# Routing from pairs of score columns, and dense loads tied to the gathers, in a two-layer attention and expert kernel

## The chip, the cores and the metric

One core of a Trainium2 chip runs the whole kernel. The metric is the device time of one execution in microseconds, as a median over runs. Engines are named as in the profile: PE (matmul), PEld (its weight load), DVE, ACT, POOL, SP (which only issues DMAs here).

## The reference

Two layers over 256 tokens of width 1024, float32. Each layer has a norm, attention and a gated short convolution, merged and projected, and then `peer`, which holds most of the bytes:

```python
q = (hf @ w_query).reshape(T, 8, 2, 128)
scores = einsum("thpd,hpnd->thpn", q, sub_keys)          # two score columns of 128 keys per head
top_v, top_i = top_k(scores, 16)
cand_v = top_v[:, :, 0, :, None] + top_v[:, :, 1, None, :]
cand_i = top_i[:, :, 0, :, None] * 128 + top_i[:, :, 1, None, :]
best_v, best_pos = top_k(cand_v.reshape(T, 8, 256), 16)
expert_idx = take_along_axis(cand_i, best_pos)           # 128 experts of 16384 per token
gates = softmax(best_v)
a = gelu(einsum("td,thkd->thk", h, expert_u[expert_idx]))
out = einsum("thk,thkd->td", gates * a, expert_v[expert_idx])
```

The output of the second layer is normed once more.

## The kernel before

The 256 tokens are two blocks of 128, block 0 and block 1 (`t` in the code). The expert stage (`experts`) does them in two ways at once.

**Block 0, dense.** All 16384 rows of `expert_u` and then of `expert_v` are streamed through SBUF, 64 MiB each. "An expert" in the loops is a group of 128 rows; a load brings a pair of them, 1 MiB. The U loop multiplies each pair with the hidden state (L1079) and leaves gelu values in `halves` (tiles `al` and `ah`). `weigh` makes one-hot tiles from the transposed factors iT, jT and gT (POOL, ACT and DVE, L1048 to L1052), multiplies them on PE (L1066), and scales `halves` with the result on DVE (L1068). The V loop multiplies `halves` with each pair of V (L1124), into two PSUM tiles that collect over all 128 steps. `factors` makes iT, jT and gT with three PE transposes (L889) and three DVE copies; their PSUM tile has two buffers.

**Block 1, gathered.** For each of a token's 128 experts one indirect DMA on POOL's queue (L977) brings a row per token, 128 x 1024 (0.52 MB): 128 gathers from U and 128 from V, in the order of GROUPS. They land in 8 row buffers (9 in the first and 11 in the second layer from the middle of the V loop on). `use` consumes the oldest: DVE, L993 for U (dot product with the token's h) or L1001 for V (adds to y1), and the freed buffer is gathered into at once. A group can be gathered when its indices are routed.

**Routing** (`route`, a generator in the list `bg`) is some 17 us of DVE per block and quarter of the heads: MAX, MAX_INDEX and MATCH_REPLACE over four score columns of 128 keys (L825 to L829), the sums (L835), a second search (L842 to L846), and one-hot products that give indices (L851 to L873). `route_all` does block 1's four quarters, then block 0's, then the shares and `factors`. `query` makes 16 units of the queries on PE (L926), the scores of a unit one unit later (L911), and after every fourth unit ACT copies four score columns of each block from PSUM to `s4` (L916) and hands them to `route_all`.

**The order of the work** is the order in which the program is written: each engine does its instructions in that order and waits on semaphores. `fill(budget)` lets `route_all` go on by so much estimated time per step of the query and U loops, with a credit of at most 3000. In the V loop the number of uses per step is set so that the remaining gathers fall evenly to LAST = 10 at the end.

**Loads.** `load_ahead` issues the next load of `stream` on SP's queue as soon as the program has a free buffer for it: one of three `raw` buffers, or, for the query weights and U, spare parts of tiles that are not yet in use (`al`, `ah`, `rows`, `hot`). SP then waits until the buffer's last reader is done. The stream goes on without a break into the weights of the next layer.

After the V loop, `update` adds y times a gate row to x for block 0, the last ten gathers are used, then `update` for block 1, the transposes of x for the next layer (`turn_x`), and in the second layer the final norm and output per block.

## Time and profile before

| what | us |
| --- | --- |
| median of 3 runs | 1887.41 (1883.96 to 1890.22) |
| the profiled execution, its own time | 1891.51 |
| its span | 1889.7 |
| busy: PE / DVE / POOL / ACT | 1610.9 / 1404.6 / 889.1 / 572.9 |
| bytes moved | 669.21 MB, mean 354 GB/s over the span |

The span has a part for each layer. Layer 0: mixing until about 255, query and routing from there, the U loop from about 325 to 623, the V loop to 926, the rest until 970. Layer 1 repeats it: query from about 1178, U loop to about 1550, V loop to 1847, end at 1889.7. Busy time of an engine is a share over all these stages. A stage is read by what was late in it: the rate of the DMA engines in a stretch, and the wait ahead of an instruction, which stands in brackets behind its row with the instruction that ended it.

### The profile page before, as it was taken

The page shows a single profiled execution, that of the slowest core. Times are in us where ns is not written, and L with a number is a line of the kernel's source. Part 1 is how long each engine was busy: PE and PEld are TensorE (multiplying, and loading weights), DVE is VectorE, ACT ScalarE, POOL GpSimd, SP SyncE. Part 2 cuts the span into 40 slices and gives each one's busy share as a digit, 9 for nine tenths or more (in the row PEclk, how much of TensorE's full clock was granted, in tenths as well). Part 3 has the DMA queues.
Part 4 walks back from the last instruction along what each step waited for, and adds up shares of the span by engine and source line. Part 5 has one row for each costly group of instructions (what it writes and reads, how often), then busy time and mean ns, then how long its engine had stood idle before and what let it go on. Part 6 is the DMA issues. An engine that isn't in the chain of part 4 may idle for free.

```text
span 1889.7 us, 25904 instructions
## 1 busy us (share of the span) xinstructions
PE 1610.9 (85%) x9524; PEld 1261.0 (67%) x9527; DVE 1404.6 (74%) x2603; ACT 572.9 (30%) x1241; POOL 889.1 (47%) x731
## 2 busy tenths in 40 slices
PE   6798889978589999899559999999785999997990
PEld 4688768978589755433247997899775995453330
DVE  7897848999988766643586967499999885666338
ACT  3464232111166444200045444121113654440001
POOL 3424203444488745544551231144436985555443
PEclk7999989989889999899879999999887999998995
DMA  8658787999999999999935677799999999999995
GB/s 317 247 208 301 268 333 291 404 408 408 400 354 400 412 416 416 409 415 417 412 132 200 238 298 260 295 397 409 409 409 352 404 403 416 416 415 415 417 416 230
DMA packets 162960, 669.21 MB, mean 354 GB/s; under 512 B 15761, under 2 KB 15761, under 8 KB 146450
## 3 DMA queue, kind: packets, MB, share of 16 engines
q1 hardware_dynamic: 87106, 396.39, 53.7%
q0 software_dynamic: 73856, 268.48, 35.9%
q10 hardware_dynamic: 1872, 2.69, 0.5%
q8 instruction: 75, 1.23, 0.3%
q14 instruction: 51, 0.42, 0.1%
HBM read 666.46 MB, written 1.05 MB: 353 GB/s over the span
## 4 chain that ended last, share of the span: by engine, by line
DMA 34%; DVE 30%; PE 22%; issue 5%; POOL 2%; ACT 2%; POOLq 0%; DVEq 0%; ACTq 0%; SPq 0%
DMA rows<-in_expert_v_dram,idx 20%; DMA rows<-in_expert_rows_dram,idx 11%; PE mm L1079 8%; DVE rows L993 7%; DVE y L1001 6%; PE mm L926 3%; PE wp L1066 3%; DVE raw L280 2%; DVE wl L335 2%; PE mm L384 1%; PE mm L385 1%; PE mm L386 1%; POOL rows L977 1%; DMA raw<-in_w_gt_dram 1%; DVE ti L826 1%
## 5 line engine op out<-in xcount | busy, mean ns | idle before, releaser
L1001 DVE SCALAR_TENSOR_TENSOR y<-rows,cv,y 128x1024 f32<-128x1024 f32 x254 | 337.4, 1328 | 198.1 <-DMA rows<-in_expert_v_dram,idx 190.3
L977 POOL DMA_INDIRECT rows<-in_expert_rows_dram,idx x256 | 287.7, 1124 | 359.8 <-DVE rows L993 133.3
L977 POOL DMA_INDIRECT rows<-in_expert_v_dram,idx x256 | 304.2, 1188 | 317.6 <-DMA rows<-in_expert_v_dram,idx 137.2
L993 DVE SCALAR_TENSOR_TENSOR rows<-rows,h 128x1024 f32<-128x1024 f32 x256 | 325.4, 1283 | 73.9 <-DMA rows<-in_expert_rows_dram,idx 66.3
L335 POOL TENSOR_TENSOR wl<-raw,wh 128x1024 fp32r<-128x1024 f32 x52 | 134.3, 2587 | 258.6 <-ACT wh L330 249.3
L1079 PE MATMUL mm<-hfull,raw 128*128 128x128 f32 x1984 | 242.2, 282 | 15.0 <-ACT al L1093 15.0
L1124 PE MATMUL yp<-raw,ah 128*128 128x512 f32 x512 | 239.1, 612 | 17.7 <-DMA raw<-in_expert_v_dram 14.8
L1079 PEld LDWEIGHTS mm<-hfull,raw 128*128 128x128 f32 x1984 | 234.2, 197 | 15.8 <-ACT al L1093 15.8
L1124 PE MATMUL yp<-raw,al 128*128 128x512 f32 x512 | 237.5, 607 | 2.1 <-DMA raw<-in_expert_v_dram 2.0
L1051 ACT ACTIVATE hot<-iotf,iT 128x128 f32<-128x128 f32 x512 | 163.3, 390 | 200.8 <-PE wp L1066 175.1
L1079 PE MATMUL mm<-hfull,ah 128*128 128x128 f32 x1600 | 193.7, 283 | 31.6 <-ACT al L1093 23.6
L1079 PEld LDWEIGHTS mm<-hfull,ah 128*128 128x128 f32 x1600 | 189.5, 199 | 32.8 <-ACT al L1093 24.3
L1124 PEld LDWEIGHTS yp<-raw,ah 128*128 128x128 f32 x512 | 94.2, 193 | 160.9 <-issue 97.7
L1066 PEld LDWEIGHTS wp<-hot 128*128 128x128 f32 x1024 | 131.4, 196 | 60.7 <-POOL hot L1049 39.6
L384 PE MATMUL mm<-hh,wh 128*128 128x256 f32 x512 | 149.9, 293 | 14.0 <-ACT gt L770 6.1
L1124 PEld LDWEIGHTS yp<-raw,al 128*128 128x128 f32 x512 | 93.5, 193 | 99.8 <-issue 94.8
L1066 PE MATMUL wp<-hot 128*128 128x64 f32 x1024 | 133.5, 274 | 27.2 <-POOL hot L1049 27.1
L330 ACT ACTIVATE wh<-raw 128x1024 fp32r<-128x1024 f32 x112 | 116.1, 1053 | 113.9 <-DMA raw<-in_w_gt_dram 47.6
L385 PE MATMUL mm<-hl,wh 128*128 128x256 f32 x512 | 146.3, 286 | 0.0
L386 PE MATMUL mm<-hh,wl 128*128 128x256 f32 x512 | 146.2, 286 | 0.0
L1049 POOL TENSOR_TENSOR hot<-hot,gT 128x256 f32<-128x256 f32 x128 | 137.3, 1073 | 2.3
L335 DVE TENSOR_TENSOR wl<-raw,wh 128x1024 fp32r<-128x1024 f32 x60 | 91.3, 1531 | 41.2 <-ACT wh L330 40.3
(229 smaller groups left out, 2345.3 us busy)
## 6 DMA issues: line engine op xcount, KB each, us to landing
raw<-in_expert_v_dram SPq DMA_DIRECT2D x128, 1024.0 KB
raw<-in_expert_u_dram SPq DMA_DIRECT2D x62, 1024.0 KB
ah<-in_expert_u_dram SPq DMA_DIRECT2D x50, 1024.0 KB
raw<-in_w_adat_dram SPq DMA_DIRECT2D x64, 512.0 KB
raw<-in_w_gt_dram SPq DMA_DIRECT2D x16, 1024.0 KB
raw<-in_w_adag_dram SPq DMA_DIRECT2D x16, 1024.0 KB
raw<-in_w_cv_dram SPq DMA_DIRECT2D x12, 1024.0 KB
raw<-in_w_qk_dram SPq DMA_DIRECT2D x8, 1024.0 KB
```

Of the source, the lines that this page charges most:

```text
L335: l_engine().tensor_tensor(lo, raw, f(h), op=OP.subtract)
L384: T.matmul(ps, h[:, c], mh[:, k], start=first, stop=False)
L385: T.matmul(ps, h[:, c], ml[:, k], start=False, stop=False)
L386: T.matmul(ps, lo[:, c], mh[:, k], start=False, stop=last)
L977: G.indirect_dma_start(out=t, out_offset=None, in_=rows[kind], in_offset=bass.IndirectOffsetOnAxis(ap=idx[:, s:s + 1], axis=0))
L993: V.scalar_tensor_tensor(t, t, 1.0, h1, op0=OP.mult, op1=OP.mult, accum_out=av[:, s:s + 1])
L1001: V.scalar_tensor_tensor(y1, t, cv[:, s:s + 1], y1, op0=OP.mult, op1=OP.add)
L1049: G.tensor_tensor(q, q, gT[:, ts, None].to_broadcast([128, TB, 64]), op=OP.mult)
L1051: A.activation(p[:, i], iotf, AF.Abs, bias=iT[:, b * TB + i:b * TB + i + 1])
L1066: T.matmul(ps[:, t], p[:, t], q[:, t], start=True, stop=True)
L1079: T.matmul(ps[:, u + x], raw[:, x, k * 128:(k + 1) * 128], hf[:, k, :128], start=(k == 0), stop=(k == KD - 1))
L1124: T.matmul(ys[q], halves[i // 64][:, i % 64], raw[:, x, q * 512:(q + 1) * 512], start=(i == 0), stop=(i == NE - 1))
```

## The change

Five edits, all in or around `experts`.

- `query` collects scores in PSUM tiles of two columns, copies them after every second unit, and hands `route_all` the tile with its first two columns. `route` does these two, then yields until the other two are there (`whole`).
- `fill` has a credit of 4000; the query loop gives 3600 per step before step 9 and 2400 from there on (2600 before).
- Between the shares and `factors` of block 0 the generator yields eight more times.
- While gathers are left (`in_step`), each V load of the stream is preceded by a DVE memset of one element and a DMA of one element over it on SP's queue, so that SP comes to the load only when DVE has come to the memset.
- All gathers are used by step 122 of the V loop; block 1 is then updated (and in the second layer normed and put out), and block 0 last. `turn_x` takes block 1 first.

```diff
-LAST = 10
+LAST = 122
...
+    in_step = {"on": False, "n": 0, "marks": cst.tile([1, DEPTH * NE // 2], F32, name="marks")}
...
+            if kind == "V" and in_step["on"]:
+
+                mark = in_step["marks"][0:1, in_step["n"]:in_step["n"] + 1]
+                in_step["n"] += 1
+                V.memset(mark, 0.0)
+                nc.sync.dma_start(mark, d["c"][:, 0:1])
             for s, ap in parts:
                 nc.sync.dma_start(t[:, s], ap)
...
-        credit[0] = min(credit[0] + budget, 3000.0)
+        credit[0] = min(credit[0] + budget, 4000.0)
...
         for i in range(4):
+            while i == 2 and not whole():
+                yield None
             s = s4[:, i]
...
         def score(n, qs):
+            if n % 2 == 0:
+                for t in range(NT):
+                    banks[t] = w_ps([128, 2, 128])
             if n % 4 == 0:
-                for t in range(NT):
-                    banks[t] = w_ps([128, 4, 128])
                 banks["k"] = keys.popleft()
...
-            if n % 4 == 3:
+            if n % 2:
                 for t in (1, 0):
-                    s4 = pool.tile([128, 4, 128], F32, name=f"sc{t}", bufs=4 - 2 * t)
-                    A.activation(s4, banks[t], AF.Copy)
-                    got(t, n // 4, s4)
+                    if n % 4 == 1:
+                        s4s[t] = pool.tile([128, 4, 128], F32, name=f"sc{t}", bufs=4 - 2 * t)
+                    A.activation(s4s[t][:, n % 4 - 1:n % 4 + 1], banks[t], AF.Copy)
+                    got(t, n // 4, s4s[t], n % 4 == 3)
...
             shares(rp, sel[0], slice(0, 8))
             yield 600
+            for _ in range(8):
+                yield None
             factors(sel[0], iT, jT, gT)
...
-            fill(2600)
+            fill(3600 if n < 9 else 2400)
...
+        def finish_block(t, last_t):
+            update(tail, ys, row, t, xg, last_t)
+            if xg:
+                y, ops = rstd_ops(t, t + 1)
+                for op in ops:
+                    op()
+                scale(xg[0], t, y, V, A)
...
-                while len(tasks) + len(flying) > LAST + (left - LAST) * (1 - (i + 1) / NE):
+                while len(tasks) + len(flying) > left * (1 - (i + 1) / LAST):
                     if not flying:
                         break
                     use()
+                in_step["on"] = bool(tasks or flying)
                 tick()
             dense_done()
-        xg = None
-        if fg is not None:
-            xg = tail.tile([128, NT, D], F32, name="xg"), fg
+            if e == LAST:
+                assert not flying
+                finish_block(1, 0)
         pol["pool"] = 1.0
-        for t in range(NT):
-            while t and flying:
-                use()
-            update(tail, ys, row, t, xg, 1)
...
+        finish_block(0, 0)
...
-        xps = None if xg else turn_x()
+        xps = None if xg else turn_x((1, 0))
```

**DVE around the factors of block 0, layer 0.** `sel` holds the routed factors and gates, `y` is y1; a row with `y` is one use of a V gather. Before:

```order
644 L867 TENSOR_REDUCE sel_2402<-oh 128x32
645 L1001 SCALAR_TENSOR_TENSOR y_2407<-rows_2326,cv,y_2407 128x1024
646 L1001 SCALAR_TENSOR_TENSOR y_2407<-rows_2323,cv,y_2407 128x1024
647 L1001 SCALAR_TENSOR_TENSOR y_2407<-rows_2324,cv,y_2407 128x1024
648 L1001 SCALAR_TENSOR_TENSOR y_2407<-rows_2325,cv,y_2407 128x1024
649 L1001 SCALAR_TENSOR_TENSOR y_2407<-rows_2326,cv,y_2407 128x1024
650 L881 TENSOR_REDUCE sm<-sel_2402 128x8
651 L882 RECIPROCAL sm<-sm 128x8
652 L883 TENSOR_TENSOR sel_2402<-sel_2402,sm 128x128
653 L893 TENSOR_SCALAR iT<-wp 128x128
654 L891 COPY jT<-wp 128x128
655 L891 COPY gT<-wp 128x128
```

With the change, from the shares on:

```order
645 L891 TENSOR_REDUCE sm<-sel_2403 128x8
646 L892 RECIPROCAL sm<-sm 128x8
647 L893 TENSOR_TENSOR sel_2403<-sel_2403,sm 128x128
648 L1013 SCALAR_TENSOR_TENSOR y_2408<-rows_2327,cv,y_2408 128x1024
649 L1013 SCALAR_TENSOR_TENSOR y_2408<-rows_2324,cv,y_2408 128x1024
650 L1013 SCALAR_TENSOR_TENSOR y_2408<-rows_2325,cv,y_2408 128x1024
651 L1013 SCALAR_TENSOR_TENSOR y_2408<-rows_2326,cv,y_2408 128x1024
652 L1013 SCALAR_TENSOR_TENSOR y_2408<-rows_2327,cv,y_2408 128x1024
653 L1013 SCALAR_TENSOR_TENSOR y_2408<-rows_2324,cv,y_2408 128x1024
654 L1013 SCALAR_TENSOR_TENSOR y_2408<-rows_2325,cv,y_2408 128x1024
655 L1013 SCALAR_TENSOR_TENSOR y_2408<-rows_2326,cv,y_2408 128x1024
656 L903 TENSOR_SCALAR iT<-wp 128x128
```

The copies of the factors stand behind eight more uses; from the start of routing there are 87 uses ahead of them before, and 90 now. On PE the three transposes stand behind 83 experts of the U loop (eight products each). Before:

```order
1322 L1079 MATMUL mm<-hfull,ah 128x128 x48
1323 L1079 MATMUL mm<-hfull,raw 128x128 x40
1324 L889 MATMUL wp<-ident,sel_2402 128x128 x3
1325 L1079 MATMUL mm<-hfull,raw 128x128 x8
1326 L1079 MATMUL mm<-hfull,ah 128x128 x8
1327 L1066 MATMUL wp<-hot 128x64 x4
```

With the change:

```order
1322 L1097 MATMUL mm<-hfull,ah 128x128 x48
1323 L1097 MATMUL mm<-hfull,raw 128x128 x48
1324 L1097 MATMUL mm<-hfull,ah 128x128 x8
1325 L899 MATMUL wp<-ident,sel_2403 128x128 x3
1326 L1097 MATMUL mm<-hfull,ah 128x128 x16
1327 L1084 MATMUL wp<-hot 128x64 x4
```

They stand behind 85 experts with the change, two more.

**DVE at the end of layer 0.** `tmp<-yp` and the row behind it are the update of block 0, `tmp<-y` that of block 1. Before, from the last row of the update of block 0 on:

```order
950 L442 TENSOR_TENSOR xt<-xt,tmp 128x512
951 L1001 SCALAR_TENSOR_TENSOR y_2407<-rows_2323,cv,y_2407 128x1024
952 L1001 SCALAR_TENSOR_TENSOR y_2407<-rows_2324,cv,y_2407 128x1024
953 L1001 SCALAR_TENSOR_TENSOR y_2407<-rows_2325,cv,y_2407 128x1024
954 L1001 SCALAR_TENSOR_TENSOR y_2407<-rows_2326,cv,y_2407 128x1024
955 L1001 SCALAR_TENSOR_TENSOR y_2407<-rows_2323,cv,y_2407 128x1024
956 L1001 SCALAR_TENSOR_TENSOR y_2407<-rows_2324,cv,y_2407 128x1024
957 L1001 SCALAR_TENSOR_TENSOR y_2407<-rows_5708,cv,y_2407 128x1024
958 L1001 SCALAR_TENSOR_TENSOR y_2407<-rows_2325,cv,y_2407 128x1024
959 L1001 SCALAR_TENSOR_TENSOR y_2407<-rows_2326,cv,y_2407 128x1024
960 L1001 SCALAR_TENSOR_TENSOR y_2407<-rows_2323,cv,y_2407 128x1024
961 L438 TENSOR_TENSOR tmp<-y_2407,row 128x512
```

Ten uses stand between the two updates. With the change, with the memsets of the last tied loads:

```order
1013 L195 MEMSET marks 1x1
1014 L1013 SCALAR_TENSOR_TENSOR y_2408<-rows_2327,cv,y_2408 128x1024
1015 L1013 SCALAR_TENSOR_TENSOR y_2408<-rows_2324,cv,y_2408 128x1024
1016 L195 MEMSET marks 1x1
1017 L1013 SCALAR_TENSOR_TENSOR y_2408<-rows_2325,cv,y_2408 128x1024
1018 L446 TENSOR_TENSOR tmp<-y_2408,row 128x512
1019 L450 TENSOR_TENSOR xt<-xt,tmp 128x512
1020 L446 TENSOR_TENSOR tmp<-y_2408,row 128x512
1021 L450 TENSOR_TENSOR xt<-xt,tmp 128x512
1022 L446 TENSOR_TENSOR tmp<-yp,row 128x512
1023 L450 TENSOR_TENSOR xt<-xt,tmp 128x512
```

Every pair of V steps has two uses and one memset on DVE, block 1 is updated behind the last use, and block 0 behind it. On SP each of 60 V loads per layer stands behind a one-element DMA; the last load of a layer has none.

## Rows read from the trace of the kernel before

**Rows 1.** Page, part 2: GB/s in 40 equal slices of the span.

```profile
GB/s 317 247 208 301 268 333 291 404 408 408 400 354 400 412 416 416 409 415 417 412 132 200 238 298 260 295 397 409 409 409 352 404 403 416 416 415 415 417 416 230
```

**Rows 2.** Stretches: length, busy PE PEld DVE ACT POOL (instructions), PEclk, DMA share, GB/s.

```profile
350.00:500.00 150.00, 126.40 (x1076) 125.45 (x1076) 142.25 (x401) 23.45 (x33) 67.37 (x59) 0.93 1.03 408
625.00:795.00 170.00, 157.36 (x622) 91.25 (x620) 107.44 (x165) 62.62 (x164) 95.15 (x98) 0.96 1.02 415
795.00:925.00 130.00, 120.77 (x265) 48.71 (x265) 58.42 (x52) 2.91 (x5) 58.69 (x45) 0.98 1.02 414
```

**Rows 3.** Stretches ahead of the first gather, layers 0 and 1.

```profile
290.00:300.00 10.00, 10.00 (x54) 8.97 (x53) 9.30 (x32) 2.24 (x5) 0.78 (x1) 1.00 0.03 12
1210.00:1220.00 10.00, 10.00 (x54) 8.95 (x53) 8.45 (x30) 2.24 (x5) 1.45 (x2) 1.00 0.02 5
```

**Rows 4.** Timeline of DVE, start of routing: start, length, instruction [idle before <-releaser].

```profile
280.70 0.30 DVE L825 MAX8 tv<-sc 128x8 f32<-128x128 f32 x1 [20.14 <-ACT sc L916]
...
284.13 0.28 DVE L825 MAX8 tv<-sc 128x8 f32<-128x128 f32 x1
...
303.50 1.22 DVE L993 SCALAR_TENSOR_TENSOR rows<-rows,h 128x1024 f32<-128x1024 f32 x1 [3.57 <-PE mm L926]
```

**Rows 5.** Timeline of POOL: the first gather of layer 0.

```profile
299.22 1.01 POOL L977 DMA_INDIRECT rows<-in_expert_rows_dram,idx  x1 [54.56 <-DVE sc L827]
```

**Rows 6.** Timeline of PE around the transposes, layer 0.

```profile
495.01 9.10 PE L1079 MATMUL mm<-hfull,raw 128*128 128x128 f32 x80
...
526.37 0.45 PE L889 MATMUL wp<-ident,sel 128*128 128x128 f32 x1 [7.05 <-DVE iT L893]
```

**Rows 7.** Timeline of DVE in the same place.

```profile
518.71 6.56 DVE L1001 SCALAR_TENSOR_TENSOR y<-rows,cv,y 128x1024 f32<-128x1024 f32 x5
...
525.94 0.28 DVE L893 TENSOR_SCALAR iT<-wp 128x128 f32<-128x128 f32 x1
```

**Rows 8.** Stretches of 40 us around the transposes, layers 0 and 1.

```profile
510.00:550.00 40.00, 24.58 (x196) 24.02 (x197) 34.80 (x51) 18.91 (x47) 27.09 (x24) 0.74 0.93 335
1430.00:1470.00 40.00, 25.21 (x207) 24.66 (x208) 35.71 (x51) 19.98 (x51) 27.25 (x25) 0.77 0.92 341
```

**Rows 9.** Groups by line, 625 to 795: busy, mean ns | idle before, releasers.

```profile
L1001 DVE SCALAR_TENSOR_TENSOR y<-rows,cv,y 128x1024 f32<-128x1024 f32 x32 | 43.4, 1355 | 25.2 <-DMA rows<-in_expert_v_dram,idx 23.3 <-issue 1.7
L993 DVE SCALAR_TENSOR_TENSOR rows<-rows,h 128x1024 f32<-128x1024 f32 x31 | 40.2, 1301 | 31.7 <-DMA rows<-in_expert_rows_dram,idx 31.6
```

**Rows 10.** Groups by line, 795 to 925.

```profile
L1001 DVE SCALAR_TENSOR_TENSOR y<-rows,cv,y 128x1024 f32<-128x1024 f32 x43 | 55.2, 1284 | 68.5 <-DMA rows<-in_expert_v_dram,idx 68.2
```

**Rows 11.** Timeline of PE: the last two pairs of V, layer 0.

```profile
918.46 7.47 PE L1124 MATMUL yp<-raw,ah 128*128 128x512 f32 x16 [0.53 <-DMA raw<-in_expert_v_dram]
```

**Rows 12.** Timeline of SP's queue: the next layer's first loads.

```profile
917.97 0.38 SPq L190 DMA_DIRECT2D raw<-in_w_qk_dram  x1
922.20 4.14 SPq L190 DMA_DIRECT2D raw<-in_w_v_dram  x2
...
956.00 28.37 SPq L190 DMA_DIRECT2D raw<-in_w_qk_dram  x2
```

**Rows 13.** Stretches behind the V loop of layer 0.

```profile
925.00:950.00 25.00, 3.14 (x11) 1.54 (x9) 18.70 (x17) 2.71 (x6) 15.26 (x13) 0.60 1.03 409
950.00:965.00 15.00, 0.00 (x0) 0.00 (x0) 14.69 (x9) 0.63 (x1) 7.73 (x3) 0.50 0.53 200
```

**Rows 14.** Timeline of DVE: the last of four updates of x, layer 0.

```profile
967.06 0.69 DVE L442 TENSOR_TENSOR xt<-xt,tmp 128x512 f32<-128x512 f32 x1
```

**Rows 15.** Page, part 5: ACT's copies of weights.

```profile
L330 ACT ACTIVATE wh<-raw 128x1024 fp32r<-128x1024 f32 x112 | 116.1, 1053 | 113.9 <-DMA raw<-in_w_gt_dram 47.6
```

**Rows 16.** Chain that ended last, 975 to 1000: start, length, what.

```profile
984.00 4.78 DMA raw<-in_w_qk_dram
```

**Rows 17.** Timeline of DVE: the last ten uses, layer 1.

```profile
1865.33 13.17 DVE L1001 SCALAR_TENSOR_TENSOR y<-rows,cv,y 128x1024 f32<-128x1024 f32 x10
```

**Rows 18.** Stretch in which the last gather of layer 1 lands.

```profile
1864.00:1868.00 4.00, 0.00 (x0) 0.00 (x0) 3.64 (x8) 0.77 (x2) 0.00 (x0) 0.50 0.89 358
```

More of the change, by code (lines that the diff above doesn't have):

```diff
@@ L815, in across, with route @@
                 T.matmul(ys[2 * t + q], sl[:, ts], h[:, c], start=False, stop=last)
-    def route(pool, t, q, s4, sel, l, idx):
+    def route(pool, t, q, s4, sel, l, idx, whole):
         tv = pool.tile([128, 4, 16], F32, name="tv", bufs=2)
@@ L902, in query @@
         pend = None
-        banks = {}
+        banks, s4s = {}, {}
         def score(n, qs):
+            if n % 2 == 0:
+                for t in range(NT):
+                    banks[t] = w_ps([128, 2, 128])
             if n % 4 == 0:
-                for t in range(NT):
-                    banks[t] = w_ps([128, 4, 128])
                 banks["k"] = keys.popleft()
             for t in range(NT):
-                T.matmul(banks[t][:, n % 4], qs[:, t * 128:(t + 1) * 128], banks["k"][:, n % 4],
+                T.matmul(banks[t][:, n % 2], qs[:, t * 128:(t + 1) * 128], banks["k"][:, n % 4],
                          start=True, stop=True)
-            if n % 4 == 3:
+            if n % 2:
                 for t in (1, 0):
-                    s4 = pool.tile([128, 4, 128], F32, name=f"sc{t}", bufs=4 - 2 * t)
-                    A.activation(s4, banks[t], AF.Copy)
-                    got(t, n // 4, s4)
+                    if n % 4 == 1:
+                        s4s[t] = pool.tile([128, 4, 128], F32, name=f"sc{t}", bufs=4 - 2 * t)
+                    A.activation(s4s[t][:, n % 4 - 1:n % 4 + 1], banks[t], AF.Copy)
+                    got(t, n // 4, s4s[t], n % 4 == 3)
         for n in range(16):
@@ L1009, in experts @@
         scores = {}
+        whole = set()
         def route_all():
@@ L1015, in route_all @@
                         yield None
-                    yield from route(rp, t, q, scores.pop((t, q)), sel[t], l, idx if t else None)
+                    yield from route(rp, t, q, scores[t, q], sel[t], l, idx if t else None,
+                                     lambda: (t, q) in whole)
                     if t:
@@ L1022, in route_all, with got @@
             yield 600
+            for _ in range(8):
+                yield None
             factors(sel[0], iT, jT, gT)
             yield 1500
-        def got(t, q, s4):
+        def got(t, q, s4, last):
             scores[t, q] = s4
+            if last:
+                whole.add((t, q))
         def step(n):
-            fill(2600)
+            fill(3600 if n < 9 else 2400)
             issue()
@@ L1102, in experts @@
         left = len(tasks) + len(flying)
+        in_step["on"] = True
+        xg = None
+        def finish_block(t, last_t):
[5 more added lines that the diff above has]
+                scale(xg[0], t, y, V, A)
         for e in range(0, NE, 2):
@@ L1117, in experts @@
                 row = gate_row(tail, l, 1)
-            if e == 122:
+                if fg is not None:
+                    xg = tail.tile([128, NT, D], F32, name="xg"), fg
+            if e == 120:
                 warm_sqrt()
@@ L1131, in experts @@
                     use()
+                in_step["on"] = bool(tasks or flying)
                 tick()
             dense_done()
-        xg = None
-        if fg is not None:
-            xg = tail.tile([128, NT, D], F32, name="xg"), fg
+            if e == LAST:
+                assert not flying
+                finish_block(1, 0)
         pol["pool"] = 1.0
-        for t in range(NT):
-            while t and flying:
-                use()
-            update(tail, ys, row, t, xg, 1)
-            if xg:
-                y, ops = rstd_ops(t, t + 1)
-                for op in ops:
-                    op()
-                scale(xg[0], t, y, V, A)
-            elif t == 0:
-                while len(ready) < 2 and next_unit():
-                    pass
-        xps = None if xg else turn_x()
+        finish_block(0, 0)
+        if not xg:
+            while len(ready) < 2 and next_unit():
+                pass
+        xps = None if xg else turn_x((1, 0))
         es.close()
```

## The prediction

> **What bounds the kernel now.** I read the page's row of GB/s first, then stretches, then single queues. From slice 8 to 20 and from 27 to 39 the DMA engines move 397 to 417 GB/s, with one dip each to 354 and 352 [rows 1]: these are the expert stages of the two layers. A table by stretch shows the same without the slices' edges: 408 GB/s while routing runs, 415 and 414 in the two halves of the V stage, while PE has idle time in all three [rows 2]. The reader is to see that in these stages no engine is the limit, but the bytes: 64 MiB of dense U, 64 MiB of dense V and 256 gathers of 0.52 MB per layer. The bytes are the same after the change. So it can gain only where the DMA engines stand idle inside a stage, or where work stands between the last byte and the next stage; and it can lose wherever it makes them idle.
>
> There are three such places per layer. **Before the first gather**: 10 us at 12 and 5 GB/s [rows 3]; dense U has filled every free buffer, and no index is ready. **At the transposes of the factors**: 40 us at 335 and 341 GB/s [rows 8]. **At the end**: 15 us at 200 GB/s after layer 0 [rows 13], and in layer 1 13.2 us of DVE alone after the last gather has landed [rows 17, 18].
>
> **Start.** The first MAX waits for the scores of four columns until 280.70; two columns take DVE until 284.13, 3.43 us [rows 4]. With pairs these two are done about two query units earlier, while DVE idles (20.14 us before the first MAX), and the rest begins when it did before. Indices and the first gather, 299.22 [rows 5], come 3.4 us earlier: 6.9 us for both layers. In DVE's order three more column blocks now stand ahead of the first use of a gather, where it waited 3.57 us [rows 4]: DVE is then 7.0 us ahead altogether. Bounds: 0 (the first gathers wait for something else) and 6.9. The four more activations per eight units stand in ACT's idle time.
>
> **Transposes.** PE comes to them at 504.1 and ends the third at 526.8 [rows 6]; the third needs DVE's copy of the first (two PSUM buffers), so PE is held until DVE gets there, at 525.94 [rows 7]. By the order, PE now does two more experts before (80 records of five took 9.10 us [rows 6]: 3.6 us), and DVE has 90 uses before its copies in place of 87 (1.31 us each [rows 7]: 3.9 us later), but is 7.0 us ahead: 525.9 + 3.9 - 7.0 = 522.8. The hold is then 15.5 us, not 22.3. What matters more is what DVE does in it: 12 uses in a row, each freeing a row buffer every 1.31 us, which asks 0.52 MB / 1.31 us = 400 GB/s of gathers. So the DMA engines stay busy while no dense buffer comes free. The dip is worth (409 - 335) / 409 x 40 = 7.2 us in layer 0 and 6.7 in layer 1 [rows 8, 13]; I keep about 2 us of each for the restart of the dense loads and take 5.0 per layer, 10.0 in all. Bounds: 0 (the hold only moves) and 13.9.
>
> **The tie.** 60 memsets per layer, each shorter than the 0.28 us of a 128x128 copy [rows 7], so under 17 us of DVE, which idles 63 and 72 us in the two halves [rows 2]; 60 small DMAs at 0.38 us of SP each [rows 12], with nothing else in SP's queue than the loads they hold. Load g+3 now leaves only after DVE has done the uses of pair g. Behind it wait the following loads, and PE. Two uses per pair are in the order, so a pair is 1.05 + 2 x 0.524 = 2.10 MB, 5.07 us at 414 GB/s, against 4.06 us per dense pair in the second half now (130 us for 32). Dense gets slower, gathers faster, the sum of bytes is the same: I cost it at 0. What hides it is that gathers take what dense leaves: with no dense load left they moved 409 GB/s alone [rows 13]. If that cover is gone, see the third rival. Nearest rows for the ring of three pairs: a load alone 4.78 us [rows 16], PE 3.7 per pair [rows 11], two uses 2.6, issue 0.4: 11.5 us, and the one-hot products on top in the first half, against 15.2 us for three pairs: the ring has room, of less than 3.7 us.
>
> The Trainium skill, page "DMA: Bandwidth & Descriptors", section "Anatomy of one DMA", gives every DMA about 2.0 us besides its bytes. Did a load stand behind the landing of its small DMA, that would use up more than half of this room, by an estimate from that figure; the order has the load wait only for PE and for an older DMA of its slot, so the sum by that page is the same unless the queue itself serializes them. No run here shows a 4-byte load.
>
> **Ends.** Before, ten gathers were left to be used after token block 0. Now they go first, and what comes last is the dense part: PE 3.73 us per pair [rows 11]. Once load 60 has landed, PE needs 4 x 3.73 = 14.9 us for pairs 60 to 63, while the three loads behind take 3.15 MB / 409 = 7.7 us at full rate: PE ends 7.2 us after the point at which the bytes could have landed. (Load 63 leaves when pair 60 is done, lands 3.7 + 4.8 = 8.5 us after load 60: in time.)
> Layer 0: at 950 the DMA engines still owed 3.0 MB [rows 13] less one load of the next layer issued at 956.00 [rows 12] = 1.95 MB = 4.8 us, and they had carried three loads of the next layer before (917.97, 922.20 [rows 12]) = 7.7 us, which now stand behind V. 950 + 4.8 - 7.7 + 7.2 = 954.3; the update adds 4 x 0.69 = 2.8 [rows 14], two weight copies on ACT that the gathers used to hide 2.1 [rows 15]: 959.2 against 967.75 [rows 14], 8.5 us. The next layer's first loads leave later, but two pairs before PE ends, so they land first.
> Layer 1: 1864 to 1868 moved 1.43 MB, 0.52 of it output [rows 18]: last gather near 1866.2. 1866.2 + 7.2 = 1873.4, where the last update now starts at 1878.5 [rows 17]: 5.1 us.
> Bounds: 0 (bytes and PE leave the end where it is) and 17.75 (all from 950 to 967.75) plus 12.3 (1866.2 to 1878.5).
>
> **Sum.** 6.9 + 10.0 + 8.5 + 5.1 = 30.5 us. The profiled execution took 1891.5, so 1861.0; it lies 4.1 above the median of the runs shown (1887.4), so **1857** for the median.
>
> **Rivals.**
> 1. Only the ends pay: DVE is 95% busy from 350 to 500 [rows 2], so three microseconds at its start may be lost in waits for landings, and the third transpose still waits for DVE. Against it: the 10 us of idle DMA before the first gather are plain. Gain 13.6: 1874.
> 2. The bytes fill the gaps anyway: a start of 3 us is paid back, the ends are given back by the next layer's loads, which come later (984.00 is a load that PE's chain waits for [rows 16]). Then within 5.7 us: 1885. The chain after 984 hangs on buffers freed after the norm, not on the loads moved, which speaks against it.
> 3. Slower: the tie holds dense back and the gathers don't take the room. Place: the V stages, 60 pairs per layer. Gathers were used at 63 in 170 us and 43 in 130 us [rows 9, 10], 2.70 and 3.02 us each; if that rate stays, a pair takes 5.40 and 6.05 us in place of 5.07: (0.33 + 0.98) x 30 x 2 layers = 79 us, and the time is 1857 + 79 = 1936. It decides from 5.07 + 30.5 / 120 = 5.32 us per pair on. For it: 55 and 68 us in which DVE waits for landings. Against it: these waits are there because dense loads took most of the rate, and 409 GB/s from gathers alone.
>
> **How the numbers follow.** Forecast 0.60, rival 1 0.18, rival 2 0.09, rival 3 0.13. Faster by over 0.3% (5.7 us, about what a measurement of this kernel can tell from no change): forecast and rival 1, 0.78; within 0.3%: 0.09; slower: 0.13. The range must leave out no more than 0.2: below, transposes at their upper bound (3.9 more) and ends better by some 10 give 1843; above, it takes in rival 1 and rival 2 in part, to 1884. The likeliest case alone, with a third of its gain more or less: 1847 to 1867.
>
> **What would show it.** Right: first gather 3 to 4 us earlier after the query stage begins; the transposes' dip at 390 GB/s or more; V loads at 5.0 to 5.1 us each with 410 or more GB/s; the last use of a gather before the last dense product, and no DVE uses after it. Wrong: V stretches under 405 GB/s or over 5.3 us per pair (rival 3); a hold of PE that is as long as before with the same dip (rival 1); layer 1's first products that wait longer for their weights (rival 2).

## The result and the profile after

| | before | after |
| --- | --- | --- |
| median, us | 1888.05 (1883.96 to 1890.22, 4 runs) | 1863.97 (1858.32 to 1870.19, 4 runs) |
| ratio, 95% interval | | 0.9876, 0.984 to 0.9912 |
| profiled execution / its span | 1891.51 / 1889.7 | 1870.19 / 1868.4 |
| the same two kernels in a later, longer measurement | 1886.39 (9 runs) | 1862.27 (5 runs), 0.9882, 0.9864 to 0.99 |

Faster by 22 to 24 us, where 30.5 were forecast; 1857 stood on record, in a range of 1843 to 1884. The runs below are held against the later measurement, 0.9882, since it has their precision; 0.001 of ratio is 1.9 us, and an interval is about 3.5 us to either side, so that the difference of two of these ratios is uncertain by about 5 us.

The page of after, part 2, and the same stretches and rows as before, in the order of the prediction. In the slices, the low one in each expert stage stands at 391 and 382 in place of 354 and 352 [rows 1], and now has a neighbour that is low too, 392 and 389:

```profile
GB/s 318 252 193 320 260 336 307 404 408 409 408 391 392 409 415 416 415 415 414 410 169 198 251 288 256 327 384 408 409 404 382 389 402 415 411 416 414 415 416 283
```

Timelines of POOL, PE, DVE and SP, layer 0 (start, length, instruction, idle ahead and its releaser). POOL, the first gather [rows 5]; PE at the transposes [rows 6]; DVE between the shares and the copies [rows 7]:

```profile
294.24 1.01 POOL L989 DMA_INDIRECT rows<-in_expert_rows_dram,idx  x1 [49.71 <-DVE sc L837]
...
523.73 0.48 PE L899 MATMUL wp<-ident,sel 128*128 128x128 f32 x1 [16.10 <-DVE iT L903]
...
507.96 0.29 DVE L893 TENSOR_TENSOR sel<-sel,sm 128x128 f32<-128x128 f32 x1
508.17 3.92 DVE L1013 SCALAR_TENSOR_TENSOR y<-rows,cv,y 128x1024 f32<-128x1024 f32 x3
512.57 1.28 DVE L1013 SCALAR_TENSOR_TENSOR y<-rows,cv,y 128x1024 f32<-128x1024 f32 x1 [0.49 <-DMA rows<-in_expert_v_dram,idx]
515.29 1.28 DVE L1013 SCALAR_TENSOR_TENSOR y<-rows,cv,y 128x1024 f32<-128x1024 f32 x1 [1.44 <-DMA rows<-in_expert_v_dram,idx]
517.85 1.28 DVE L1013 SCALAR_TENSOR_TENSOR y<-rows,cv,y 128x1024 f32<-128x1024 f32 x1 [1.28 <-DMA rows<-in_expert_v_dram,idx]
520.57 1.28 DVE L1013 SCALAR_TENSOR_TENSOR y<-rows,cv,y 128x1024 f32<-128x1024 f32 x1 [1.44 <-DMA rows<-in_expert_v_dram,idx]
522.18 1.28 DVE L1013 SCALAR_TENSOR_TENSOR y<-rows,cv,y 128x1024 f32<-128x1024 f32 x1 [0.33 <-DMA rows<-in_expert_v_dram,idx]
523.39 0.28 DVE L903 TENSOR_SCALAR iT<-wp 128x128 f32<-128x128 f32 x1
```

The first gather follows the first product of the query stage by 37.0 us (257.22 to 294.24), before by 40.7 (258.49 to 299.22). PE was held 16.1 us. DVE had eight uses between shares and copies, and in five of them it waited for a landing.

Stretches of the V stage and its end (length, busy PE PEld DVE ACT POOL, PEclk, DMA share, GB/s) [rows 2, 13]; SP's queue and DVE in it, one pair; PE's last pairs [rows 11]; DVE's last update of block 0 [rows 14]:

```profile
650.00:800.00 150.00, 134.29 (x467) 74.15 (x467) 102.52 (x181) 52.90 (x140) 108.27 (x89) 0.96 1.02 415
800.00:925.00 125.00, 101.12 (x215) 40.36 (x214) 64.62 (x79) 2.68 (x4) 65.11 (x48) 0.97 1.02 415
925.00:950.00 25.00, 21.84 (x62) 9.69 (x61) 11.78 (x15) 2.47 (x7) 0.00 (x0) 1.00 0.89 325
```

```profile
909.48 0.06 DVE L195 MEMSET marks<- 1x1 f32 x1
...
909.59 0.24 SPq L196 DMA_DIRECT2D marks<-in_c_dram  x1
909.92 0.33 SPq L198 DMA_DIRECT2D raw<-in_expert_v_dram  x1
...
937.11 10.57 PE L1155 MATMUL yp<-raw,ah 128*128 128x512 f32 x24 [0.58 <-DMA raw<-in_expert_v_dram]
...
948.91 0.69 DVE L450 TENSOR_TENSOR xt<-xt,tmp 128x512 f32<-128x512 f32 x1
```

A pair takes 5.04 us (904.87 to 935.11 for six), at 415 GB/s; the load leaves 0.33 us after the DMA of one element. The last three pairs run on PE without a wait, and x is complete at 949.60, before at 967.75. But the first product of layer 1's norm comes 12.3 us later and not 5.8. DVE in between, then POOL:

```profile
950.45 0.16 DVE L482 SCALAR_TENSOR_TENSOR ss<-ss 128x2 f32<-128x2 f32 x1 [0.85 <-ACT sq L408]
952.44 0.17 DVE L484 RECIPROCAL ss<-ss 128x2 f32<-128x2 f32 x1 [1.83 <-ACT ss L483]
952.63 1.17 DVE L485 SCALAR_TENSOR_TENSOR ss<-ss 128x2 f32<-128x2 f32 x1
953.84 2.26 DVE L486 TENSOR_TENSOR ss<-ss 128x2 f32<-128x2 f32 x1
956.14 2.26 DVE L487 SCALAR_TENSOR_TENSOR ss<-ss 128x2 f32<-128x2 f32 x1
...
951.44 6.94 POOL L343 TENSOR_TENSOR wl<-raw,wh 128x1024 fp32r<-128x1024 f32 x3 [33.56 <-ACT wh L338]
```

The three small operations took 0.16 us each before (969.52 to 970.07). Two rows of DVE before, the reciprocal and the second of the three:

```profile
969.32 0.17 DVE L476 RECIPROCAL ss<-ss 128x2 f32<-128x2 f32 x1 [0.27 <-ACT ss L475]
969.71 0.16 DVE L478 TENSOR_TENSOR ss<-ss 128x2 f32<-128x2 f32 x1
```

Now they take 1.17, 2.26 and 2.26, 5.2 us more, and each ends within 0.05 us of the end of one of POOL's three subtractions (953.75, 956.07, 958.38, if the 6.94 us are three times 2.31). The reciprocal ahead of them waited 1.83 us for the square root, which stood on ACT behind two weight copies; before it waited 0.27.

To see where time went, each profiled execution is cut at instructions: from the first product of the query stage to x complete in layer 0 (A), from there to the next norm's first product (N), from there to the next query stage (M, which the change doesn't touch), and from that to the end (B). What lies ahead of A is not touched either; it takes 258.5 us before, 257.2 after and 253.2 to 257.8 in the others. All kernels of this study, in us:

| | A | N | M | B | ratio |
| --- | --- | --- | --- | --- | --- |
| before | 709.3 | 5.8 | 204.1 | 712.0 | 1 |
| after | 692.4 | 12.3 | 203.2 | 703.3 | 0.9876 |
| after, again | 691.1 | 12.4 | 201.4 | 700.7 | 0.9882 |
| routing_only | 702.8 | 5.1 | 203.6 | 707.7 | 0.9949 |
| ends_only | 696.4 | 12.4 | 199.4 | 709.3 | 0.9940 |
| fours | 695.0 | 12.4 | 201.3 | 701.4 | 0.9889 |
| no_delay | 693.8 | 12.4 | 202.7 | 704.8 | 0.9905 |
| no_tie | 699.8 | 12.4 | 199.4 | 705.5 | 0.9931 |
| act_copies | 696.7 | 12.4 | 202.4 | 703.4 | 0.9917 |
| last_124 | 691.4 | 12.4 | 201.6 | 703.2 | 0.9871 |
| wl_halves | 692.5 | 10.1 | 202.8 | 700.8 | 0.9866 |
| wl_dve | 689.5 | 6.1 | 203.1 | 702.1 | 0.9858 |
| wl_last | 691.5 | 6.1 | 203.7 | 701.2 | 0.9847 |
| wl_last_delay | 697.1 | 6.2 | 197.9 | 706.1 | 0.9899 |

M, the same code throughout, spreads from 197.9 to 204.1: a difference of a few microseconds in one cell says little by itself. The two profiles of after differ by 1.3 in A and 2.6 in B.

### The profile page after: what moved, and what is told of

Read it like the earlier page. It is cut to its first block, busy times and chain, and to the rows that moved or that the text cites. A ratio compares the mean times of both kernels' runs of the same rounds, so it can differ in the third digit from the quotient of the medians.

```text
span 1868.4 us, 26270 instructions
## 1 busy us (share of the span) xinstructions
PE 1620.5 (87%) x9527; PEld 1270.3 (68%) x9527; DVE 1414.8 (76%) x2723; ACT 575.8 (31%) x1257; POOL 951.1 (51%) x731
## 3 DMA queue, kind: packets, MB, share of 16 engines
q8 instruction: 75, 1.23, 0.3%
## 4 chain that ended last, share of the span: by engine, by line
DVE 33%; DMA 29%; PE 23%; issue 6%; POOL 4%; ACT 3%; SPq 0%; POOLq 0%; ACTq 0%; DVEq 0%
DMA rows<-in_expert_v_dram,idx 16%; PE mm L1097 8%; DVE rows L1005 7%; DMA raw<-in_expert_v_dram 6%; PE yp L1155 4%; DVE raw L288 4%; DMA rows<-in_expert_rows_dram,idx 4%; PE wp L1084 3%; DVE y L1013 3%; POOL rows L989 3%; DVE wl L343 2%; PE mm L392 1%; PE mm L393 1%; PE mm L394 1%; PE mm L938 1%
## 5 line engine op out<-in xcount | busy, mean ns | idle before, releaser
L989 POOL DMA_INDIRECT rows<-in_expert_rows_dram,idx x256 | 306.8, 1198 | 335.3 <-DVE rows L1005 92.2
L989 POOL DMA_INDIRECT rows<-in_expert_v_dram,idx x256 | 329.4, 1287 | 231.5 <-DMA rows<-in_expert_v_dram,idx 95.7
L1005 DVE SCALAR_TENSOR_TENSOR rows<-rows,h 128x1024 f32<-128x1024 f32 x256 | 329.2, 1303 | 3.5 <-DMA rows<-in_expert_rows_dram,idx 3.3
L1155 PE MATMUL yp<-raw,al 128*128 128x512 f32 x512 | 244.4, 622 | 32.1 <-DMA raw<-in_expert_v_dram 31.8
L1097 PEld LDWEIGHTS mm<-hfull,raw 128*128 128x128 f32 x1984 | 232.5, 196 | 19.9 <-ACT al L1111 15.8
L392 PE MATMUL mm<-hh,wh 128*128 128x256 f32 x512 | 150.4, 294 | 10.1 <-ACT qT L656 6.3
L1067 POOL TENSOR_TENSOR hot<-hot,gT 128x256 f32<-128x256 f32 x128 | 152.2, 1190 | 2.4
L1084 PE MATMUL wp<-hot 128*128 128x64 f32 x1024 | 129.1, 270 | 2.9 <-POOL hot L1067 2.9
```

Source lines behind the costliest of these rows:

```text
L392: T.matmul(ps, h[:, c], mh[:, k], start=first, stop=False)
L989: G.indirect_dma_start(out=t, out_offset=None, in_=rows[kind], in_offset=bass.IndirectOffsetOnAxis(ap=idx[:, s:s + 1], axis=0))
L1005: V.scalar_tensor_tensor(t, t, 1.0, h1, op0=OP.mult, op1=OP.mult, accum_out=av[:, s:s + 1])
L1067: G.tensor_tensor(q, q, gT[:, ts, None].to_broadcast([128, TB, 64]), op=OP.mult)
L1084: T.matmul(ps[:, t], p[:, t], q[:, t], start=True, stop=True)
L1097: T.matmul(ps[:, u + x], raw[:, x, k * 128:(k + 1) * 128], hf[:, k, :128], start=(k == 0), stop=(k == KD - 1))
```

## The experiments

**The changed kernel once more (after_again).** No edit.

> The changed kernel as it is, once more, so that the runs that undo or add one part have a base of the same precision. If its first measurement stands: 1862 to 1866 us, ratio 0.986 to 0.989; from query to x of layer 0 about 692 us, from query to the end of layer 1 about 703 us, 12.3 us from x to the next norm's first product. If it comes out under 1861 us, the tie and the delay are worth more and the mended copies less than the other runs were read to say; over 1867 us, the other way round.

1862.27 us, 0.9882 (0.9864 to 0.99), inside what was expected. The first measurement stands.

**Routing alone (routing_only)** and **ends alone (ends_only)**. The first is the kernel before with the edits of `route`, `query`, `route_all` and `fill`; the second the changed kernel with these undone:

```diff
-            if n % 2:
+            if n % 4 == 3:
...
-            for _ in range(8):
-                yield None
             factors(sel[0], iT, jT, gT)
...
-            fill(3600 if n < 9 else 2400)
+            fill(2600)
```

> The kernel before with the routing part of the change alone (pairs of columns, delay, budgets): block 0 first at the end of each V stage, ten gathers left, no tie. Theory (the ends gave 10.2 us in layer 0, less 6.5 us that the next norm lost, and 6.1 us in layer 1): 9.8 us more than the changed kernel, 1872 to 1876 us; the next norm's first product again about 6 us after x is complete. Forecast's own size of the ends: 13.6 us, 1878 us. Rival (routing gives nothing, the ends all of it): 1884 to 1890 us.

> The changed kernel with both parts of the routing change undone (scores in fours, no delay, budgets of before); ends and marks as changed. Theory (pairs and delay act on one thing, how far PE is ahead of DVE when it comes to the transposes, so that either alone gives most of what both give): by stages both together were worth 6.4 us in layer 0 and 4.3 us in layer 1 between the kernel before and the one with routing alone, so 10 to 11 us more than the changed kernel, 1873 to 1876 us. Rival (the two add up): undone singly they cost 1.5 and 4 us, so 1868 to 1871 us.

0.9949 (0.9931 to 0.9967) and 0.9940 (0.9923 to 0.9957): routing alone is worth 9.6 us, ends alone 11.3, both 22.3. The two halves add up within the uncertainty. Routing on top of the ends is 10.9 us, the ends on top of routing 12.6. In time routing_only lies at 1876.9 us, 0.9 above its theory's range, and ends_only at 1875.0 us, in the range of the theory that pairs and delay act on one thing, and above that of the rival, 1868 to 1871.

**Scores in fours (fours)** and **no delay (no_delay)**: one routing edit undone at a time, as in the diff above (no_delay: the yields and the budgets).

> The changed kernel with the scores copied in fours again, all else as changed. Theory (pairs bring the first gather 3.4 to 3.7 us earlier per layer, of which 1.2 to 1.6 us are lost again within 40 us): first gather 3.5 us later after the query stage begins, the whole 4 to 6 us longer, 1868 to 1870 us. Forecast's own size: 6.9 us, 1871 us. Rival (a start a few us earlier is paid back by waits for landings): 1862 to 1866 us.

> The changed kernel without the eight steps of delay before the transposes of the factors and with the budgets of before (2600 per unit, 3000 at most). Theory (PE comes to the transposes earlier, DVE to their copies not as much, PE's hold is 20 us or more again and the DMA engines dip): by bytes moved the late transposes are worth 4.1 us in layer 0 and 1.9 us in layer 1, so 1868 to 1871 us. Forecast's own size: 10.0 us, 1874 us. Rival (the dip only moves): 1862 to 1866 us.

0.9889 (0.9867 to 0.9911) and 0.9905 (0.9883 to 0.9928): 1.3 and 4.3 us over the changed kernel, neither clear of noise. fours has the time of its rival (an early start is paid back), and no_delay lies at the edge of its theory. Against ends_only, the delay alone (that is fours) gives 9.6 us, pairs alone (no_delay) 6.6: 16.2 together, where both at once give 10.9. In fours the first gather is 40.7 us behind the query's first product again, 3.7 later. Yet the stretch 20 to 40 us behind the first gather differs; of after and of fours, layers 0 and 1:

```profile
314.00:334.00 20.00, 19.91 (x150) 18.92 (x149) 19.17 (x65) 4.08 (x9) 7.60 (x8) 1.00 0.95 351
1222.00:1242.00 20.00, 19.91 (x150) 18.95 (x149) 19.17 (x65) 4.08 (x9) 7.61 (x7) 1.00 0.97 355
```

```profile
318.00:338.00 20.00, 19.91 (x164) 19.30 (x163) 19.21 (x60) 4.45 (x9) 7.82 (x7) 1.00 1.02 405
1227.00:1247.00 20.00, 19.91 (x164) 19.33 (x164) 19.17 (x60) 4.66 (x8) 8.06 (x8) 1.00 1.02 408
```

351 and 355 GB/s against 405 and 408. (405 - 351) / 409 x 20 = 2.6 us of each early start of 3.7 us are lost again here. DVE has under 1 us of idle time in it: routing and uses together fill it, and it comes to seven uses in the stretch of after and to eight in that of fours, so row buffers come free no faster. The dense loads leave no earlier either: the first one in these stretches leaves 64.0 us behind the query's first product in both (321.18 and 321.50).

The delay is not the same in the two. By the records of PE and DVE the transposes stand behind 88 experts and 93 uses in fours, behind 85 and 90 in the changed kernel; in no_delay behind 80 and 85, in ends_only, as before, behind 83 and 87. And PE is held at the transposes for only 6.6 us in fours (4.8 in layer 1), because it was held just ahead of them. PE, then ACT:

```profile
509.32 10.23 PE L1095 MATMUL mm<-hfull,raw 128*128 128x128 f32 x64 [9.18 <-ACT ah L1109]
533.49 0.48 PE L899 MATMUL wp<-ident,sel 128*128 128x128 f32 x1 [6.58 <-DVE iT L903]
...
507.13 0.23 ACT L862 ACTIVATE sel<-sel 128x32 f32<-128x32 f32 x1 [19.35 <-DVE sel L861]
```

The gelu that PE waits for stands on ACT behind the exponential of routing, and that one waited 19.35 us for DVE. Together PE's two waits are 15.8 us in fours (14.2 in layer 1), and 17.6 in the changed kernel (1.5 and 16.1; 17.1 in layer 1).

**The copies of the factors on ACT (act_copies).**

```diff
-            if i:
-                V.tensor_copy(o, ps)
-            else:
-                V.tensor_scalar(o, ps, -1.0, None, op0=OP.mult)
+            A.activation(o, ps, AF.Copy, scale=1.0 if i else -1.0)
```

> The changed kernel with the three copies of the transposed factors on ACT, not on DVE, so that PE's third transpose doesn't wait for DVE's queue. Theory (PE's hold makes the dip): the hold falls from 16 us to under 7 us (DVE's shares are still ahead of the third), the DMA engines stay at 405 GB/s or more in the 60 us behind, where they now miss 4.0 us in layer 0 and 5.4 us in layer 1; the whole 4 to 9 us less, 1855 to 1860 us. Rival (the dip comes from DVE, which falls behind with uses, one-hots and products of the shares, not from PE): the dip is there all the same, 1862 to 1866 us.

Slower than the changed kernel by 6.6 us: 0.9917 (0.9904 to 0.9931), so the theory is wrong, and the time of the rival was missed too. PE's timeline:

```profile
506.68 0.30 PE L899 MATMUL wp<-ident,sel 128*128 128x128 f32 x1 [0.77 <-DVE sel L893]
...
528.95 1.97 PE L1081 MATMUL wp<-hot 128*128 128x64 f32 x8 [18.40 <-POOL hot L1064]
```

The transposes no longer wait, and PE stands 18.4 us at the first one-hot product, two experts of the U loop later (the row names POOL, which got its one-hots from DVE behind the same uses). So the place of the hold is not what matters: PE is ahead of DVE by 15 to 18 us at the end of routing, and waits at the first thing it needs from DVE, here as in fours. The dip behind it does not go, as the rival had it:

```profile
532.00:542.00 10.00, 10.00 (x75) 10.00 (x75) 5.58 (x8) 4.54 (x12) 5.30 (x5) 0.80 0.70 242
...
562.00:572.00 10.00, 10.00 (x92) 10.00 (x91) 7.79 (x15) 6.38 (x17) 8.46 (x7) 1.00 0.96 348
```

Why it is deeper than in the changed kernel was not settled.

**Sixteen steps of delay (wl_last_delay)**, on the kernel of the last experiment below.

> The kernel of the run before it with a delay of 16 steps, not 8, before the transposes. Theory (the hold is PE's lead over DVE): PE comes to them four products of experts later and DVE eight uses later at most, the hold falls from 16 us to 8 to 12 us, the dips of 2 to 5 us behind get smaller by 1 to 2 us per layer: 1853 to 1857 us. Rival (PE is then the bound of the rest of the U stage, since the one-hot products stand in fewer steps): the dip moves to the end of the U stage, 1857 to 1862 us.

0.9899 (0.9877 to 0.9921), 9.8 us over the same kernel with eight, where a gain was expected. PE:

```profile
541.13 0.48 PE L903 MATMUL wp<-ident,sel 128*128 128x128 f32 x1 [21.05 <-DVE iT L907]
```

The hold grew, to 21.1 us. Eight more steps put eight more experts ahead of the transposes, not four products, and brought PE there 15.6 us later (504.1 to 519.7), and DVE to the copies 20.4 us later (iT's release, 520.7 to 541.1): 1.95 and 2.55 us a step, for DVE's uses wait for landings there, as in the rows of after. A longer delay widens PE's lead.

**Without the tie (no_tie).**

```diff
-        in_step["on"] = True
+        in_step["on"] = False
...
-                in_step["on"] = bool(tasks or flying)
+                in_step["on"] = False
```

> The changed kernel (1864.0 us) without the marks: loads of the second matrix no longer wait for the uses of the gathers; all else as changed. Theory (the tie costs nothing and holds dense back so that the gathers end first): without it dense pairs of the second half of the V stage take about 4.1 us again and not 5.03, the last uses of gathers come after the last dense product in both layers, and the three first loads of the next layer again go ahead of gathers in layer 0; x of layer 0 is complete 3 to 8 us later, the whole 1867 to 1878 us. Rival (the order of the blocks makes the gain, the tie none of it): 1861 to 1866 us. Rival (the tie costs time, since PE stands 1.3 us per pair): under 1860 us.

0.9931 (0.9907 to 0.9955): 9.2 us over the changed kernel. SP's queue, PE and DVE at the end of layer 0:

```profile
915.01 4.09 SPq L198 DMA_DIRECT2D raw<-in_expert_v_dram  x2
922.55 0.38 SPq L198 DMA_DIRECT2D raw<-in_w_qk_dram  x1
926.77 4.14 SPq L198 DMA_DIRECT2D raw<-in_w_v_dram  x2
...
924.43 6.08 PE L1155 MATMUL yp<-raw,ah 128*128 128x512 f32 x13
...
942.62 9.21 DVE L1013 SCALAR_TENSOR_TENSOR y<-rows,cv,y 128x1024 f32<-128x1024 f32 x7 [0.16 <-DMA rows<-in_expert_v_dram,idx]
...
956.64 0.69 DVE L450 TENSOR_TENSOR xt<-xt,tmp 128x512 f32<-128x512 f32 x1
```

Dense ends at 930.5 and three loads of the next layer leave, all ahead of the last gathers, whose uses end at 951.8. x is complete 7.4 us later than in the changed kernel by A (8.7 against its second profile). Dense pairs leave every 4.1 us again (ten loads in 36.76 us from 882.35 on), as expected. The tie is what keeps the gathers from being last.

**The low parts of the next weights off POOL (wl_dve)** and **in halves on POOL (wl_halves)**. The first puts their copies on ACT ahead of the last update and the subtractions on DVE; the second only cuts POOL's instructions in two:

```diff
+        if defer is not None:
+            defer.append(lambda: V.tensor_tensor(lo, raw, f(h), op=OP.subtract))
...
+        if not xg:
+            while len(ready) < 2 and next_unit(low_parts):
+                pass
         finish_block(0, 0)
-        if not xg:
-            while len(ready) < 2 and next_unit():
-                pass
+        if not xg:
+            low_parts.popleft()()
...
-        rr = rms_row()
+        rr = rms_row(lambda: low_parts.popleft()())
```

```diff
-        l_engine().tensor_tensor(lo, raw, f(h), op=OP.subtract)
+            for q in range(2):
+                c = slice(q * 512, (q + 1) * 512)
+                e.tensor_tensor(lo[:, c], raw[:, c], f(h)[:, c], op=OP.subtract)
```

> The changed kernel, with the two low parts of the first weights of layer 1 off POOL: their copies on ACT stand before the last update, one subtraction on DVE behind that update, the other on DVE while PE makes the row sums. Theory (a DVE instruction with two inputs in SBUF waits until POOL's running instruction ends): the small operations of the norm take 0.16 us each again, not 1.17, 2.26 and 2.26, the square root no longer stands behind two copies, and the first product comes 6 to 7 us after x is complete, not 12.3; the whole 5 to 6.5 us less, 1857 to 1859 us. Rival (the small operations are long for another reason, the clock or landings): 12 us as before, 1863 to 1866 us. Rival (the mixing stage then waits for its loads): first product earlier, the whole 1862 to 1866 us all the same.

> The changed kernel with each of those subtractions on POOL in two halves of 512 columns: the same work on POOL, in instructions half as long. Theory (DVE waits for the end of POOL's running instruction): the three small operations take at most 1.2 us each, in place of 1.17, 2.26 and 2.26, and the first product comes 2 to 3 us earlier after x is complete (9.5 to 10.5 us); the whole 1861 to 1863 us. Rival (the two engines share a rate while both run): the three take 5.7 us as now, no change.

0.9858 (0.9842 to 0.9873) and 0.9866 (0.9849 to 0.9882): 4.5 and 3.0 us under the changed kernel, as expected, the first at the edge of noise and the second within it; N, 12.3 or 12.4 in every run with the ends and neither of these edits, takes 6.1 and 10.1 us. DVE and POOL of wl_halves:

```profile
952.68 0.16 DVE L491 SCALAR_TENSOR_TENSOR ss<-ss 128x2 f32<-128x2 f32 x1
952.87 1.12 DVE L492 TENSOR_TENSOR ss<-ss 128x2 f32<-128x2 f32 x1
954.03 1.18 DVE L493 SCALAR_TENSOR_TENSOR ss<-ss 128x2 f32<-128x2 f32 x1
955.25 1.25 DVE L512 TENSOR_SCALAR dg<-ident,ss 128x128 f32<-128x128 f32 x1
...
951.48 7.38 POOL L347 TENSOR_TENSOR wl<-raw,wh 128x512 fp32r<-128x512 f32 x6 [33.56 <-ACT wh L338]
```

POOL's six instructions take 1.23 us each (7.38 us for six) and so end at 952.71, 953.94, 955.17, 956.40; the DVE instructions end at 953.99, 955.21 and 956.50. The same work on POOL in shorter instructions makes shorter waits: DVE waits for the end of an instruction, it doesn't share a rate. In wl_dve they take 0.16 us.

**The last use by step 124 (last_124)** and **both mends (wl_last)**: `LAST = 124`, alone and with wl_dve's edit.

> The changed kernel with the last use of a gather by expert 124, not 122. Theory (at the end PE is late: three pairs, 10.57 us, are left once the last load that competes with gathers has landed): two pairs are left, and the ends are 2 to 4 us shorter in each layer; 1856 to 1861 us. Rival (the last gathers land too late then, and block 1's update, 2.8 us of DVE, delays block 0's): 1864 to 1869 us.

> The changed kernel with the low parts of the next layer's first weights on DVE, as in the run with them there, and the last use of a gather by expert 124. Theory: the first is worth 5 to 6 us, the second 1 to 2 us, in different places: 1856 to 1859 us. Rival (the later last gather takes the copies' place behind block 1's update): 1859 to 1862 us.

0.9871 (0.9856 to 0.9886), within the uncertainty of the changed kernel: PE's last product ends 7.0 us after the last use and not 10.8 us, but the last use comes 2.8 us later behind the query's first product. wl_last takes 1858.22 us, 0.9847 (0.983 to 0.9865), 6.6 us under the changed kernel: the fastest of the study, though not clear of wl_dve.

## Why the prediction was right, and where not

The direction, the range and the places were right; the sum was 7 to 8 us too large, and two steps of the working failed.

**Start, 6.9 us.** The first gather came 3.7 us earlier in each layer, 3.4 forecast. The step that failed is that this is time gained: 2.6 us of it go back in the next 40 us, since neither uses nor dense loads come faster there.

**Transposes, 10.0 us.** The hold was forecast at 15.5 us and is 16.1, iT at 522.8 and is at 523.4 (1.9 us later, counted from the query's first product). The 40 us from 510 have 392 GB/s and layer 1's from 1410 have 377, where 390 was asked (397 and 400 in after_again). The argument for full DMA engines in the hold failed in its working (12 uses in a row, every 1.31 us): there are eight, and DVE waits for landings and takes 1.9 us a use, and the engines were full all the same, 408 GB/s from 514 to 524, for the queues were. What was left out is the time behind the hold:

```profile
514.00:524.00 10.00, 0.27 (x2) 0.28 (x2) 5.53 (x6) 0.29 (x1) 4.67 (x6) 0.50 1.02 408
534.00:594.00 60.00, 60.00 (x540) 60.00 (x539) 50.66 (x85) 39.21 (x102) 53.26 (x44) 1.00 1.00 382
1432.00:1492.00 60.00, 58.42 (x497) 58.42 (x498) 50.10 (x81) 39.73 (x105) 51.94 (x43) 0.94 0.98 373
```

PE is then busy without a gap, and (409 - 382) / 409 x 60 = 4.0 and 5.3 us are missing, which the forecast had put at about 2.

**Their sum, 16.9 us**, is the first mis-sized term: 10.9 measured. How much of each is missing shows in the bytes. Mean rate in two stretches behind the query's first product, layer 0 / layer 1, in GB/s:

| | before | ends_only | no_delay | fours | after | after, again |
| --- | --- | --- | --- | --- | --- | --- |
| start, 20 to 110 us | 344 / 343 | 349 / 349 | 358 / 357 | 349 / 349 | 353 / 353 | 355 / 356 |
| transposes, 110 to 380 us | 396 / 397 | 397 / 393 | 399 / 398 | 399 / 404 | 402 / 399 | 403 / 402 |

Put as time at 409 GB/s and over both layers (1 GB/s in the longer stretch is 0.7 us), the two profiles of after miss 4.2 and 5.2 us less than before at the start, where 6.9 were forecast, and 5.3 and 7.9 us less at the transposes, where 10.0 were. Both terms were too large.

That each alone measured nearly what was forecast, pairs 6.6 for 6.9 and the delay 9.6 for 10.0, is luck: pairs alone (no_delay against ends_only) save 3.8 us at the start and 4.6 at the transposes. They also don't add: 16.2 us alone and 10.9 together by the times, 17.0 and 9.1 to 12.7 by the bytes. The working itself lets the pairs' 7.0 us of lead shorten the hold that the delay is meant to shorten too. But a sum of four ratios is uncertain by about 7 us, each profile is one execution, and the places of the transposes differ between these kernels; so the overlap is likely, not proven.

**The tie, 0.** Right: 5.04 us per pair for 5.07, 415 GB/s, 0.06 and 0.24 us per mark. Rival 3 needed 5.32 us per pair. SP issues the load 0.33 us behind its mark; no row shows when the mark lands. The Trainium skill, page "DMA: Bandwidth & Descriptors", section "Anatomy of one DMA — SWDGE (gpsimd) path", gives a DMA of POOL's path about 2.0 us besides its bytes, where the prediction has every DMA. The marks go by SP's queue, and no run here shows that figure for them; the rate of 415 GB/s shows that it cost nothing here, and the sum stood. What the forecast did not say is that the order of the ends needs the tie: 9.2 of the ends' 12.6 us go without it.

**Ends, 8.5 and 5.1 us.** In layer 1 right: B falls by 4.4 to 7.0 us between routing_only and the two profiles of after. In layer 0 x is complete 10.5 us earlier (A, 702.8 to 692.4), where the forecast had 10.6 before "two weight copies on ACT that the gathers used to hide 2.1". That is the second step that failed. It counted ACT's copies (1.6 us, at the square root) and forgot POOL's subtractions behind them, which the ten uses had hidden as well. They came to stand beside the norm's small operations, 5.2 us, and N went from 5.8 to 12.3. wl_dve shows it: N is 6.1 us again, and 4.5 us come back. In the code the copies and subtractions of the next layer's first two weights stood behind the update of block 0, ahead of the ten uses, and stand behind the last update now; the description of the change doesn't say so. The trace of before had a row that could have warned, at the end of layer 1 (DVE, then POOL):

```profile
1861.26 2.55 DVE L474 SCALAR_TENSOR_TENSOR ss<-ss 128x1 f32<-128x1 f32 x1 [0.79 <-ACT sq L400]
...
1861.30 2.48 POOL L449 TENSOR_TENSOR xg<-xt,fg 128x512 f32<-128x512 f32 x2
```

An operation on one column took 2.55 us there, where it takes 0.16 elsewhere, and ended 0.03 us behind POOL's two.

**Rivals.** Rival 1 has a true part (2.6 of the 3.7 us at the start do get lost, and the third transpose still waits for DVE) and the wrong whole: routing is worth 10.9 us, not nothing. Rival 2 did not come: M is 203.2 us after and 204.1 before.

30.5 less 6.0 (routing, 16.9 for 10.9) and 4.4 (norm, 6.5 lost less the 2.1 counted) is 20.1; 22.3 to 23.4 were measured, and the rest is within the uncertainty.

## What to carry to other kernels

An earlier start is worth only what the stage behind it can take up. Two terms that pull at one wait are not simply to be added: ask what each is worth when the other has been done. When an engine is ahead of the one that feeds it, moving its wait to another place gains nothing by itself. When work that hid something is moved, list all that it hid, on every engine, and look at what each will then run beside. And a queue that may run ahead is held back cheaply by a mark that the slower stream writes: here one memset and one small DMA per pair were worth 9 us.

## Unexpected of the hardware

A DVE instruction of 256 elements took 2.26 us, because POOL was in the middle of an instruction that reads two tensors. The Trainium skill, page "SBUF — State Buffer", section "Who interferes with whom", says it: a DVE instruction with two inputs in SBUF contends with a POOL instruction that reads SBUF, the port pair that they share is an exclusive lock, and whoever issues first has it for the whole instruction while the other blocks. wl_halves agrees, with waits that end with POOL's instructions of 1.23 us. So do the exceptions: with one of two inputs from PSUM DVE took 0.48 us beside POOL as always, while a TENSOR_SCALAR from SBUF with one input, which the page counts among those that contend, was held too (1.25 us for 0.29). It goes the other way as well. DVE and POOL of wl_dve:

```profile
949.81 1.22 DVE L345 TENSOR_TENSOR wl<-raw,wh 128x1024 fp32r<-128x1024 f32 x1
950.95 0.42 DVE L516 COPY dg<-yp 128x256 f32<-128x256 f32 x1
951.40 0.48 DVE L610 SCALAR_TENSOR_TENSOR hf<-mm,acol,dg 128x256 f32<-128x256 f32 x1
951.92 1.46 DVE L613 TENSOR_SCALAR hh<-hf,adac 128x256 fp32r<-128x256 f32 x1
...
949.82 3.41 POOL L347 TENSOR_TENSOR wl<-raw,wh 128x1024 fp32r<-128x1024 f32 x1 [34.20 <-ACT wh L339]
```

POOL's subtraction started 0.01 us behind DVE's and took 3.41 us, 1.1 more than alone; the TENSOR_SCALAR at 951.92 then ended 0.15 us behind it, 1.46 us for 0.35.
